# Beginning of a one-core program: zero products, first projection by parts, squares on ScalarE, early norm rows, streamed tokens for beta and the decay

## The chip, the cores and the metric

The kernel runs on one core of one Trainium2 chip. The core has a matrix engine (TensorE, PE in the profile) and three engines for element-wise work: VectorE (DVE), ScalarE (ACT) and GpSimd (POOL). SyncE (SP) issues transfers. Each engine takes its instructions in the order in which the program holds them, and waits on semaphores for what other engines and transfers deliver. The metric is the time of one execution on the device in microseconds; lower is better.

## The reference

256 tokens of width 1024 pass through a hybrid layer and then, with 16 learned tokens put in front of them, through two layers of a second kind. Only the mixer of the hybrid layer is touched by the change:

```python
def hybrid_layer(x, ...):
    h = rmsnorm(x, norm_mix_w)
    proj = h @ w_in                       # 1024 -> 3*512 (q, k, v), 512 (z), 4 (beta), 4 (a), 512 (lru_x), 512 (lru_gate)
    qkv, z, b_logit, a_logit, lru_x, lru_gate = split(proj)
    qkv = silu(causal_depthwise_conv(qkv, gdn_conv_w))        # 4 taps
    q, k, v = split(qkv); q = l2norm(q); k = l2norm(k)        # 4 heads of 128
    beta = sigmoid(b_logit); g = -exp(gdn_A_log) * softplus(a_logit + gdn_dt_bias)
    o = gated_delta_rule_chunked(q, k, v, g, beta)            # a triangular solve per chunk, a state from chunk to chunk
    gdn_out = rmsnorm(o, gdn_norm_w) * silu(z)
    hr = rg_lru(causal_depthwise_conv(lru_x, lru_conv_w) + lru_conv_b, ...)   # h[t] = a[t] h[t-1] + sqrt(1 - a[t]^2) i[t] x[t], two sigmoid gates
    lru_out = hr * gelu(lru_gate)
    x = x + concat(gdn_out, lru_out) @ w_out
    return x + square(relu(rmsnorm(x, norm_mlp_w) @ w_ff1)) @ w_ff2
```

The second block has, twice, a SwiGLU MLP, a mixer of attention and convolution, and another SwiGLU MLP.

## The kernel before, in words

**Products.** Features lie on the partitions and tokens are the 256 moving columns. Each operand is split into a rounded high part and the rest. The weights stream in by transfers on SyncE's queue into three buffers `raw`; ScalarE rounds a piece of 1024 columns to `wh`, and VectorE subtracts to get the low part `wl` (GpSimd does that for some kinds of projections, which the table `POOLED` names). Activations are held the same way: `x.hi` and `x.lo`. For each of the eight blocks of the inner dimension, `job` (line 525) issues three products into one bank of PSUM:

```python
nc.tensor.matmul(acc, h[:, s], xh, start=first and done == 0, stop=False)
nc.tensor.matmul(acc, h[:, s], xl, start=False, stop=False)
nc.tensor.matmul(acc, lo[:, s], xh, start=False, stop=last and done == total - 1)
```

One *projection* here is 24 such products, for 128 output features and all tokens. The mixer has 24 of them, in the order of `ORDER1`: four each for k, q, lru_x, lru_gate, v, z.

**Flows and the planner.** What follows a projection is written as generators (*flows*). A planner keeps an estimated clock for each engine (`clk`) and, after each step of a projection (`tick`), lets a flow go on when its inputs are due by that clock. So each engine's program order comes out of estimated costs, start values (`clk.update`), ranks of flows and limits.

**The beginning.** The tokens come into `H`. `first_norm` (line 750) makes `x.hi` on ScalarE and `x.lo` on VectorE for each of the eight blocks; the norm's factor per token is not in it, it is applied after the projections. `squares` (line 728) squares the tokens: four blocks on ScalarE, four on GpSimd, and GpSimd adds them to four accumulators. `tok_sums` (line 608) sums over features by products with a column of ones (one moving column; a float32 product takes several passes and is one or more rows in the trace), `root_norm` makes the factor `rc` per token, and `to_rows` (line 617) spreads it to a row `R`, equal on all partitions, by three products with the identity in the mask tile `M`. `R` is what each projection's result is multiplied with first.

**Behind a projection.** `conv4` (line 783) multiplies the bank with `R` into a buffer of the `arena` (a space for passing tiles, first come first served), clears the three columns ahead of it on GpSimd, lets ScalarE take the first tap and VectorE the other three (`scalar_tensor_tensor`, three *convolution steps*). `twice_silu` follows. For q and k the squares for the l2 norm are taken on GpSimd.

**The decay.** `decays` (line 885) gets beta and the decay's logit: the 16 columns `wb` (high and low part of 8 weight columns) are the moving operand and the tokens are stationary, 32 narrow products. VectorE adds the parts, a chain of small steps gives softplus, `nA` = -exp(A_log), and `G`, the log-decay per token and head. GpSimd multiplies `G` with a triangular mask into `DT`, two products spread it, and from that come the decay masks and factors of the chunks. `factors` (line 988) makes the norm factors of k and q; `bk` is the first of them, needed by the chunks.

**The chunks.** `chunk(0)` and `chunk(1)` handle 128 tokens each: transposes (*flips*) of k, the triangular matrix, its inverse in four levels of small blocks, whose last step is the 64x64 products against the masks `LM`, then U (16 products), the outputs, their root mean square `sso`, the normed output `on`, two flips back, and the gating with z into `mx`.

**The recurrence.** `lru` (line 1249) takes four tiles of lru_x: a gate product (`LG`), tanh, exponentials, a square root for all four tiles, then for each tile a multiply, a scan over tokens, a multiply with the gelu gate, and the split into `mx` (ScalarE the high part, VectorE the low).

**The end of the mixer.** w_out is applied in two halves: `o1a` the inner blocks 4 to 7 (recurrence tiles 0 to 3), 96 products into four banks, each opened by a product of zeros with 512 columns; `o1b` the blocks 0 to 3 (the chunks' output), into the same banks. From `o1b` on come the MLP and the second block.

## Time and profile before

| | us |
|---|---|
| time, median of 3 runs | 1510.01 (1508.57 to 1511.97) |
| time of the profiled execution | 1510.12 |
| its span in the profile | 1508.4 |
| TensorE busy | 98% |
| VectorE busy | 71% |
| ScalarE busy | 53% |
| GpSimd busy | 9% |

A line in a row of the profile is that of the helper that records the operation (`mm`, `tt`, `stt`, `act`, ...), "out<-in" are the program's names, and the number after the x counts instructions. A row of stretches gives for each engine its busy time with the number of instructions, then the clock granted to TensorE as a share of full speed, and what the transfers did.

### The profile page before, as it was taken

The numbers are of one execution on the slowest core, as the hardware profiler recorded it, in microseconds if no ns is written. First come the engines' busy times: TensorE is split into PE (matmuls) and PEld (weight loads), VectorE is DVE, ScalarE is ACT, GpSimd is POOL, SyncE is SP. The second block draws the span as 40 slices with busy tenths as digits, with TensorE's granted clock in tenths as the row PEclk, the third lists the DMA queues.
The fourth block names the chain that finished last, engine by engine and source line by source line (L and its number), as shares of the span: only waits on it lengthen the run. The fifth ranks groups of instructions, "written<-read, shape, count | busy, mean of one in ns | idle before, by whom it ended". The sixth has DMA issues, their size and how long they took to land. (4 is left out here: it accounts for less than half of the span.)

```text
span 1508.4 us, 29363 instructions
## 1 busy us (share of the span) xinstructions
PE 1471.4 (98%) x12130; PEld 1451.6 (96%) x12130; DVE 1073.8 (71%) x1910; ACT 800.6 (53%) x1349; POOL 136.7 (9%) x189
## 2 busy tenths in 40 slices
PE   7989999999999999999999999999999999999997
PEld 7888999999999999998999999999999989999997
DVE  5996877667666568998866655665568998876664
ACT  4568666544544445554554444544445556555552
POOL 2330300001000002231000000000002222000000
PEclk8999999999999999999999999999999999999998
DMA  5412455554644554333454444554454434555552
GB/s 207 163 57 73 164 205 190 187 200 145 209 170 176 178 177 144 144 134 112 147 214 171 173 169 161 199 185 174 165 190 155 164 113 140 184 207 196 189 183 76
DMA packets 36375, 248.57 MB, mean 165 GB/s; under 512 B 3984, under 2 KB 5264, under 8 KB 12304
## 3 DMA queue, kind: packets, MB, share of 16 engines
q1 hardware_dynamic: 35248, 245.50, 46.3%
q8 instruction: 95, 1.56, 0.4%
q10 hardware_dynamic: 992, 1.19, 0.2%
q14 instruction: 40, 0.33, 0.1%
HBM read 245.63 MB, written 1.05 MB: 164 GB/s over the span
## 5 line engine op out<-in xcount | busy, mean ns | idle before, releaser
L552 PE MATMUL bank<-x,wh 128*128 128x272 f32 (+1 forms) x2752 | 793.3, 288 | 11.0 <-ACT x L295 10.1
L553 PE MATMUL bank<-x,wh 128*128 128x272 f32 (+1 forms) x2752 | 782.8, 284 | 3.8 <-DVE x L318 2.2
L554 PE MATMUL bank<-x,wl 128*128 128x272 f32 (+1 forms) x2752 | 781.7, 284 | 4.4 <-DVE wl L307 4.4
L307 DVE TENSOR_TENSOR wl<-raw,wh 128x1024 fp32r<-128x1024 f32 (+3 forms) x467 | 546.6, 1172 | 182.7 <-PE bank L554 153.9
L295 ACT ACTIVATE wh<-raw 128x1024 fp32r<-128x1024 f32 (+4 forms) x494 | 492.1, 1001 | 255.3 <-issue 133.0
L552 PEld LDWEIGHTS bank<-x,wh 128*128 128x128 f32 x2752 | 521.5, 190 | 13.8 <-ACT x L295 10.5
L553 PEld LDWEIGHTS bank<-x,wh 128*128 128x128 f32 x2752 | 521.4, 189 | 6.9 <-DVE x L318 3.1
L554 PEld LDWEIGHTS bank<-x,wl 128*128 128x128 f32 x2752 | 521.9, 190 | 5.5 <-DVE wl L307 5.5
L554 PE MATMUL bank<-hid,wl 128*128 128x272 f32 (+1 forms) x960 | 270.5, 282 | 0.0
L552 PE MATMUL bank<-hid,wh 128*128 128x272 f32 (+1 forms) x960 | 270.5, 282 | 0.0
L553 PE MATMUL bank<-hid,wh 128*128 128x272 f32 (+1 forms) x960 | 270.5, 282 | 0.0
L553 PEld LDWEIGHTS bank<-hid,wh 128*128 128x128 f32 x960 | 180.5, 188 | 0.0
L554 PEld LDWEIGHTS bank<-hid,wl 128*128 128x128 f32 x960 | 180.5, 188 | 0.0
L552 PEld LDWEIGHTS bank<-hid,wh 128*128 128x128 f32 x960 | 180.5, 188 | 0.0
L307 DVE TENSOR_TENSOR tmp<-bank,R 128x272 f32<-128x272 f32 (+1 forms) x184 | 78.7, 429 | 63.5 <-PE bank L554 61.3
L295 ACT ACTIVATE tmp<-tmp 128x272 f32<-128x272 f32 (+1 forms) x140 | 59.4, 425 | 110.0 <-DVE tmp L307 78.0
L318 DVE SCALAR_TENSOR_TENSOR bank<-arena,C,bank 128x272 f32<-128x272 f32 (+1 forms) x232 | 102.3, 489 | 3.7 <-ACT bank L295 2.5
L510 POOL TENSOR_TENSOR wl<-raw,wh 128x1024 fp32r<-128x1024 f32 (+1 forms) x27 | 64.2, 2380 | 185.2 <-ACT wh L295 106.6
L307 DVE TENSOR_TENSOR hid<-tmp,hid 128x272 fp32r<-128x272 f32 (+1 forms) x120 | 51.7, 432 | 38.1 <-ACT hid L295 38.1
L295 ACT ACTIVATE hid<-tmp 128x272 fp32r<-128x272 f32 (+1 forms) x120 | 51.0, 426 | 42.3 <-DVE tmp L307 40.8
L295 ACT ACTIVATE x<-H,C 128x272 fp32r<-128x272 f32 (+2 forms) x64 | 30.0, 487 | 80.9 <-DVE H L307 80.3
L307 DVE TENSOR_TENSOR tmp<-tmp,bank 128x272 f32<-128x272 f32 (+1 forms) x88 | 38.0, 432 | 39.0 <-ACT tmp L295 39.0
(205 smaller groups left out, 883.2 us busy)
## 6 DMA issues: line engine op xcount, KB each, us to landing
raw<-in_w_dram SPq DMA_DIRECT2D x187, 1024.0 KB, 4.8
raw<-in_w_dram SPq DMA_DIRECT2D x32, 960.0 KB, 4.7
raw<-in_w_dram SPq DMA_DIRECT2D x16, 896.0 KB, 4.5
raw<-in_w_dram SPq DMA_DIRECT2D x2, 512.0 KB, 5.9
H<-in_xt_dram SPq DMA_DIRECT2D x1, 544.0 KB, 6.6
LG<-in_lgw_dram SPq DMA_DIRECT2D x1, 512.0 KB, 6.2
out_dram<-H SPq DMA_DIRECT2D x2, 256.0 KB, 2.2
LM<-in_cm_dram SPq DMA_DIRECT2D x1, 320.0 KB, 5.4
```

The lines of the kernel that those rows point to most:

```text
L295: nc.scalar.activation(out, in_, func, scale=scale, **kw)
L307: nc.vector.tensor_tensor(out=out, in0=a, in1=b, op=fn)
L318: nc.vector.scalar_tensor_tensor(out=out, in0=a, scalar=s, in1=b, op0=op0, op1=op1)
L510: nc.gpsimd.tensor_tensor(out=lo[:, a:a + n], in0=raw[c][:, o:o + n], in1=wh[i][:, a:a + n].bitcast(F32), op=SUB)
L552: nc.tensor.matmul(acc, h[:, s], xh, start=first and done == 0, stop=False)
L553: nc.tensor.matmul(acc, h[:, s], xl, start=False, stop=False)
L554: nc.tensor.matmul(acc, lo[:, s], xh, start=False, stop=last and done == total - 1)
```

## The change

- **Zero products.** The tile of zeros is made at the start, on 128 partitions; `WARM` = 13 products of 512 columns on it run while inputs come, and one after each of the first seven products of projection 0.
- **Projection 0 by parts.** Instead of three products per block, all eight `wh` with `x.hi`, then all eight `wl` with `x.hi`, then all eight `wh` with `x.lo`.
- **Squares on ScalarE.** All eight blocks, with no additions: `tok_sums` runs over eight accumulators instead of four. ScalarE rounds the second piece of weights ahead of them.
- **Norm rows at once.** `to_rows` is issued before the table load for exponentials and before `hrc`.
- **Streamed tokens for beta.** `wb` is now the stationary operand and the 256 tokens move, high and low, 16 products into 16 partitions; ScalarE copies the result, and two products with `two` (identity halves added) add the parts and turn the result back.
- **Decay earlier.** `decays` starts behind the first projection instead of the second and with another rank; `DT` is made on ScalarE in eight steps.
- **Convolutions.** Six fixed buffers, cleared once, instead of a new one with its own clearing; the squares of q and k go to ScalarE; the low weight parts of K and Q are no longer given to GpSimd. The pad of `hid` grows, and the planner's start values change.

```diff
--- before
+++ after
@@ -26,2 +26,4 @@
 SHARED = ("ys", "yc")
+WARM = 13
+CONVB = 6
 LEAD = 3
@@ -35,3 +37,3 @@
 AHEAD = 0.5
-POOLED = [(("a", "b", "q", "k", "v", "gc", "gs"), 4), (("yc",), 2), (("o1b",), 2), (("K", "Q"), 8)]
+POOLED = [(("a", "b", "q", "k", "v", "gc", "gs"), 4), (("yc",), 2), (("o1b",), 2)]
 LIMIT1 = 1.5
@@ -545,2 +547,15 @@
             clk["P"] = max(clk["P"], w_at[i] + LAT)
+            if u == 0:
+                for w, part in ((h, x.hi), (lo, x.hi), (h, x.lo)):
+                    for i, k in enumerate(units[u][1]):
+                        nc.tensor.matmul(
+                            acc, w[:, 128 * i:128 * i + 128], part(k), start=part == x.hi and w is h and i == 0,
+                            stop=part == x.lo and k == KD - 1,
+                        )
+                        if w is h and part == x.hi and k < KD - 1:
+                            mm(free_banks[-1], zero[:, 0:128], zero)
+                clk["P"] = 12.3
+                main.t, main.eng = clk["P"], "P"
+                tick()
+                continue
             for i, k in enumerate(units[u][1]):
@@ -702,2 +717,4 @@
     warm = const.tile([128, 1], F32, name="warm")
+    zero = pool1.tile([128, 512], BF16, name="zero")
+    nc.gpsimd.memset(zero, 0.0)
     nc.gpsimd.memset(ones, 1.0)
@@ -714,3 +731,5 @@
     emit_dma(2)
-    clk.update(P=6.5, A=4.1, V=6.2, G=5.6, D=12.0)
+    for _ in range(WARM):
+        mm(free_banks[-1], zero[:, 0:128], zero)
+    clk.update(P=6.5, A=5.3, V=6.4, G=5.6, D=12.0)
     raw_t.update({0: 3.9, 1: 9.2, 2: 12.1})
@@ -726,20 +745,15 @@
     hrc = const.tile([128, 2], F32, name="hrc")
+    two = pool1.tile([16, 8], F32, name="two")
+    convb = [arena.get(T1 + 8) for _ in range(CONVB)]
+    for a in convb:
+        nc.gpsimd.memset(a.f[:, 5:8], 0.0)
+    conv_left = [16, CONVB]
 
     def squares():
-        yield "P"
-        for k in range(4):
-            act(SQ[1].f[:, k], X(4 + k), AF.Square)
-        cur[0].t, cur[0].eng = 0.0, "P"
-        for k in range(4):
-            pt(SQ[0].f[:, k], X(k), X(k), MUL)
-        for k in range(4):
-            pt(SQ[0].f[:, k], SQ[0].f[:, k], SQ[1].f[:, k], ADD)
-        nc.gpsimd.memset(mean512, 1.0 / 512)
-        nc.gpsimd.memset(onesrow, 1.0)
+        for k in range(KD):
+            act(SQ[k // 4].f[:, k % 4], X(k), AF.Square)
         yield "P"
         yield from take()
-        root_norm([SQ[0].f[:, k] for k in range(4)], T1, rc)
+        root_norm([SQ[k // 4].f[:, k % 4] for k in range(KD)], T1, rc)
         note(ev_rc)
-        ts(hrc, rc, 0.5, MUL)
-        act(warm, ones[:, 0:1], AF.Exp)
         yield "P"
@@ -748,2 +762,4 @@
         note(ev_r1)
+        act(warm, ones[:, 0:1], AF.Exp)
+        ts(hrc, rc, 0.5, MUL)
 
@@ -759,3 +775,2 @@
     emit_high(0)
-    sq_flow = start_flow(squares())
     f = start_flow(first_norm())
@@ -766,4 +781,6 @@
         hop(f)
-    hop(sq_flow)
-    hop(sq_flow)
+    emit_high(1)
+    hop(start_flow(squares()))
+    nc.gpsimd.memset(mean512, 1.0 / 512)
+    nc.gpsimd.memset(onesrow, 1.0)
     ba = cv("w_ba").rearrange("p (a b) -> p a b", a=8)
@@ -771,2 +788,3 @@
     tt(wb[:, :, 8:16], ba, wb[:, :, 0:8].bitcast(F32), SUB)
+    tt(two, ident[0:16, 0:8], ident[0:16, 8:16], ADD)
     XR, GL = arena.get(4, T1), arena.get(4, T1)
@@ -784,5 +802,6 @@
         yield from wait(ev_r1)
-        pb = yield from room(T1 + 8)
+        while not convb:
+            yield "W"
+        pb = convb.pop(0)
         p = pb.f
-        nc.gpsimd.memset(p[:, 5:8], 0.0)
         tt(p[:, 8:8 + T1], b[:, 0:T1], R[:, 0:T1], MUL)
@@ -796,3 +815,8 @@
             stt(out, p[:, 5 + k:5 + k + T1], cv(wname, 4 * t + k), out, MUL, ADD)
-        pb.done()
+        conv_left[0] -= 1
+        if conv_left[0] < conv_left[1] or conv_left[0] < 10 and conv_left[1] > 4:
+            conv_left[1] -= 1
+            pb.done()
+        else:
+            convb.append(pb)
 
@@ -810,3 +834,3 @@
             yield from twice_silu(dst, dst)
-            pt(SQ[t // 4].f[:, t % 4], dst, dst, MUL)
+            act(SQ[t // 4].f[:, t % 4], dst, AF.Square)
             note(ev_sqk[t])
@@ -892,16 +916,17 @@
         b = free_banks.pop(0)
+        for k in range(KD):
+            mm(b[0:16, 0:T1], wb[:, k], xa.hi(k), k == 0, False)
+            mm(b[0:16, 0:T1], wb[:, k], xa.lo(k), False, k == KD - 1)
+            clk["P"] += 0.1
+        bas = yield from slot()
+        cp(bas[0:16, 0:T1], b[0:16, 0:T1])
+        yield "P"
         for c in range(2):
-            for k in range(KD):
-                mm(b[:, 16 * c:16 * c + 16], xa.hi(k)[:, hs(c)], wb[:, k], k == 0, False)
-                mm(b[:, 16 * c:16 * c + 8], xa.lo(k)[:, hs(c)], wb[:, k, 0:8], False, k == KD - 1)
+            mm(b[:, 256 + 8 * c:264 + 8 * c], bas[0:16, hs(c)], two)
+        free_tmps.append(bas)
         yield from wait(ev_rc)
-        b2 = b[:, 0:32].rearrange("p (a b c) -> p a b c", a=2, b=2)
-        ba2 = small.tile([128, 2, 8], F32, tag="ba2", name="ba2")
-        vcopy(ba2, b2[:, :, 0])
-        tt(ba2, ba2, b2[:, :, 1], ADD)
-        give(b)
-        b = ba2.rearrange("p a b -> p (a b)")
         for c in range(2):
-            stt(x12[:, 4 * c:4 * c + 4], b[:, 8 * c + 4:8 * c + 8], rc[:, c:c + 1], cv("gdn_dt_bias"), MUL, ADD)
-            act(beta[:, 4 * c:4 * c + 4], b[:, 8 * c:8 * c + 4], AF.Tanh, scale=hrc[:, c:c + 1])
+            stt(x12[:, 4 * c:4 * c + 4], b[:, 260 + 8 * c:264 + 8 * c], rc[:, c:c + 1], cv("gdn_dt_bias"), MUL, ADD)
+            act(beta[:, 4 * c:4 * c + 4], b[:, 256 + 8 * c:260 + 8 * c], AF.Tanh, scale=hrc[:, c:c + 1])
+        give(b)
         ts(x12[:, 8:12], cv("lru_a_param"), -1.0, MUL)
@@ -928,3 +953,4 @@
         for c in range(2):
-            pt(DT[c].f, bh(tri), bc(G[:, 4 * c:4 * c + 4]), MUL)
+            for h in range(4):
+                act(DT[c].f[:, h], tri, AF.Copy, scale=G[:, 4 * c + h:4 * c + h + 1])
         yield "P"
@@ -970,4 +996,2 @@
     junk = pool1.tile([128, 128], F32, name="junk")
-    zero = pool1.tile([1, 512], BF16, name="zero")
-    nc.gpsimd.memset(zero, 0.0)
 
@@ -1286,4 +1310,4 @@
         start_flow(doers[c](b, off + t), *((0, LIMIT0) if c in "kq" else (2, LIMIT1)))
-        if i == 1:
-            start_flow(decays(), 1)
+        if i == 0:
+            start_flow(decays(), 0.5)
         if i == 6:
@@ -1335,3 +1359,3 @@
         b = free_banks.pop(0)
-        mm(b, zero[:, 0:128], zero, stop=False)
+        mm(b, zero[0:1, 0:128], zero[0:1], stop=False)
         for i in range(2):
@@ -1350,3 +1374,3 @@
     phase = ExitStack()
-    hid = XS(T1, FF1, phase.enter_context(tc.tile_pool(name="ff1", bufs=1)), "hid", pad=(56, 0))
+    hid = XS(T1, FF1, phase.enter_context(tc.tile_pool(name="ff1", bufs=1)), "hid", pad=(88, 0))
 
...
```

**How the order moves.** Two places, the beginning and the first `o1a` tile, in rows of the two programs; rows in between that only repeat are left out. `x_117` and `x_118` are `x.hi` and `x.lo`, `x_119` and `x_120` those of `mx`.

TensorE at the start, before: the second and the third step of projection 1 (bank 79) with the norm's sums between them.

```order
L554 MATMUL bank_78<-x_117,wl 128x256
L552 MATMUL bank_79<-x_117,wh 128x256
L553 MATMUL bank_79<-x_118,wh 128x256
L554 MATMUL bank_79<-x_117,wl 128x256
L338 MATMUL bank_80<-ones,arena 128x1 x8
```

The same place with the change, from the last products of projection 0 to the row spread (bank 82, from `rc`).

```order
L340 MATMUL bank_85<-zero 128x512
L551 MATMUL bank_78<-x_117,wh 128x256
L551 MATMUL bank_78<-x_117,wl 128x256 x8
L551 MATMUL bank_78<-x_118,wh 128x256 x8
L567 MATMUL bank_79<-x_117,wh 128x256
L568 MATMUL bank_79<-x_118,wh 128x256
L569 MATMUL bank_79<-x_117,wl 128x256
L340 MATMUL bank_80<-ones,arena 128x1 x16
L340 MATMUL bank_81<-x_117,wb 16x256
L340 MATMUL bank_82<-M,rc 128x128
L340 MATMUL bank_82<-M,rc 128x64 x2
L340 MATMUL bank_81<-two,tmp_86 128x8 x2
```

The sums stand at the same place of projection 1, after one step of it, but there are twice as many; the products for beta and the row spread, which stood in projection 2, now stand in projection 1.

VectorE at the same time with the change: from the parts of `x.lo` to the end of the decay's chain (`sp`, `G`).

```order
L320 SCALAR_TENSOR_TENSOR x_118<-H,C,x_117 128x256 x6
L309 TENSOR_TENSOR wb<-C,wb 128x8x8
L309 TENSOR_TENSOR two<-M 16x8
L309 TENSOR_TENSOR wl<-raw,wh 128x1024 x3
L320 SCALAR_TENSOR_TENSOR rc<-rn_t,rn_y 128x2
L314 TENSOR_SCALAR hrc<-rc 128x2
L309 TENSOR_TENSOR arena<-bank_78,R 128x256
L320 SCALAR_TENSOR_TENSOR x_292<-bank_81,rc,C 128x4 x2
L309 TENSOR_TENSOR G<-sp_196,nA 128x8
L320 SCALAR_TENSOR_TENSOR arena<-arena,C 128x256 x2
```

The first multiplication with `R` has moved ahead of the decay's chain, and the second one (bank 79, not shown) stands behind it.

ScalarE with the change, from the first rounding of tokens to the exponential of the decay's chain.

```order
L297 ACTIVATE x_117<-H,C 128x256 x8
L297 ACTIVATE wh<-raw 128x1024
L297 ACTIVATE arena<-H 128x256 x8
L297 ACTIVATE wb<-C 128x8x8
L297 ACTIVATE rn_y<-bank_80,eps 128x2
L297 ACTIVATE tmp_86<-bank_81 16x256
L297 ACTIVATE R<-bank_82 128x256
L297 ACT_TABLE_LOAD
L297 ACTIVATE warm<-ones 128x1
L297 ACTIVATE arena<-arena,C 128x256
L297 ACTIVATE beta<-bank_81,hrc 128x4 x2
L297 ACTIVATE e_293<-e_293 128x12
```

Before, four squares stood here instead of eight, `R` came after the decay's `nA` instead of ahead of the table load, and no convolution stood ahead of beta.

TensorE at the first `o1a` tile, before (bank 81), from the product that opens it.

```order
L338 MATMUL bank_81<-zero 128x512
L552 MATMUL bank_81<-x_119,wh 128x256
L553 MATMUL bank_81<-x_120,wh 128x256
L554 MATMUL bank_81<-x_119,wl 128x256
L338 MATMUL bank_84<-arena 128x128 x4
L338 MATMUL bank_83<-arena 128x128 x4
L338 MATMUL bank_80<-arena 128x128 x4
L338 MATMUL bank_82<-arena 128x128 x4
L338 MATMUL bank_79<-arena 128x128 x8
L338 MATMUL bank_85<-arena 128x128 x8
```

The same place with the change (bank 79); bank 85 and bank 81 in the last rows are the two flips of the chunks' outputs.

```order
L340 MATMUL bank_79<-zero 128x512
L340 MATMUL bank_81<-arena 128x128 x4
L340 MATMUL bank_83<-arena 128x128 x4
L567 MATMUL bank_79<-x_119,wh 128x256
L340 MATMUL bank_78<-arena 128x128 x4
L340 MATMUL bank_84<-arena 128x128 x4
L340 MATMUL bank_80<-arena 128x128 x8
L567 MATMUL bank_79<-x_119,wh 128x256
L340 MATMUL bank_82<-arena 128x128 x8
L567 MATMUL bank_79<-x_119,wh 128x256
L344 MATMUL bank_85<-M,arena 128x128 x4
L344 MATMUL bank_81<-M,arena 128x128 x4
```

Before, eight steps were in the queue by the end of the second group of eight, and the flips came behind the 15th and the 17th. With the change one step stands ahead of the first eight, the third (recurrence tile 2) behind all of them, and the flips come right behind the third.

VectorE at that place with the change: `sso` is the outputs' root mean square, the last `x_120` rows are the low parts of recurrence tiles 2 and 3 (128x256) and of the two gated chunk outputs (128x4x128).

```order
L309 TENSOR_TENSOR sso<-sso,fq 128x4
L309 TENSOR_TENSOR arena<-bank_82,sso 128x512
L309 TENSOR_TENSOR arena<-bank_84,sso 128x512
L309 TENSOR_TENSOR x_120<-arena,x_119 128x256
L320 SCALAR_TENSOR_TENSOR arena<-bank_85,hw,arena 128x512
L320 SCALAR_TENSOR_TENSOR arena<-bank_81,hw,arena 128x512
L336 SCALAR_TENSOR_TENSOR arena<-arena 128x256
L309 TENSOR_TENSOR x_120<-arena,x_119 128x4x128 x2
L309 TENSOR_TENSOR x_120<-arena,x_119 128x256
L309 TENSOR_TENSOR wl<-raw,wh 128x512 x7
```

Before, all four recurrence tiles' `x_120` rows stood ahead of the first `sso` step; now tiles 2 and 3 stand among and behind the steps of the chunks' outputs. From `o1b` on the rows of TensorE are the same in both programs.

4 lines of the change are left out of this document (2 added, 2 removed).

## The prediction

> **What bounds the kernel now.** I read the page first, then the waits of TensorE, then a table of stretches, and then the rows of the queues in order of time. All times are microseconds.
>
> ```profile
> PE 1471.4 (98%) x12130; PEld 1451.6 (96%) x12130; DVE 1073.8 (71%) x1910; ACT 800.6 (53%) x1349; POOL 136.7 (9%) x189
> ```
>
> TensorE is the bound: it is busy nearly always. From the first `o1b` product on, the change leaves the order of every engine as it was, so what counts is when TensorE gets there: 163.8 (the last `zero` product at 160.69, 0.32 for it, 24 products). I split the way at three marks: the fourth projection (32.3), the end of the last 64x64 product (131.8), and `o1b` (163.8).
>
> ```profile
> core 0: us, PE busy (x) PEld busy (x) DVE busy (x) ACT busy (x) POOL busy (x), PEclk, DMA share, GB/s
> 16.10:17.50 1.40, 1.40 (x14) 1.40 (x14) 1.40 (x2) 0.73 (x1) 0.00 (x0) 1.00 0.67 94
> 18.20:23.90 5.70, 5.70 (x28) 5.70 (x29) 2.01 (x7) 2.70 (x4) 0.00 (x0) 0.50 0.75 315
> 24.40:27.60 3.20, 3.20 (x30) 3.20 (x31) 0.00 (x0) 0.00 (x0) 0.00 (x0) 1.00 0.02 5
> 27.80:31.10 3.30, 3.30 (x17) 3.30 (x16) 2.53 (x16) 0.79 (x4) 0.00 (x0) 0.50 0.00 0
> 31.70:39.40 7.70, 7.70 (x68) 7.70 (x69) 6.04 (x12) 3.60 (x6) 4.62 (x6) 1.00 0.60 221
> ...
> 67.90:131.80 63.90, 58.38 (x574) 55.44 (x572) 50.77 (x92) 46.55 (x105) 17.48 (x19) 1.00 0.23 81
> 131.80:143.10 11.30, 10.87 (x89) 10.07 (x88) 10.71 (x26) 9.11 (x20) 0.00 (x0) 1.00 0.26 94
> 143.10:152.10 9.00, 8.92 (x79) 8.69 (x78) 4.98 (x12) 7.77 (x23) 0.00 (x0) 1.00 0.33 117
> 152.10:163.80 11.70, 11.68 (x91) 10.40 (x90) 10.40 (x29) 6.71 (x18) 1.77 (x1) 1.00 0.14 34
> ```
>
> A projection product of 256 columns takes 0.113 at clock 1.00 (68 in 7.70) and 0.21 at 0.50 (27 of the 28 in 5.70). The clock drops to 0.50 after the one-column sums (16.1 to 17.5) and after the narrow `wb` products (24.4 to 27.6), though TensorE shows as busy in both, and it comes back only after several microseconds of wide products. In the last three stretches TensorE has no gap worth naming: the serial end of the two chunk flows lies under 72 projection products and the `o1a` products.
>
> ```profile
> PE bank L342 <- DVE arena L307: 2.5, 2, 1.8
> PE bank L554 <- DVE wl L307: 2.1, 2, 1.2
> ```
>
> Its waits between 32.3 and 131.8 are small: these two lead, 7.5 in all by the rows of that view. That is the most that a better fed TensorE can win there.
>
> **The change, part by part.** The sum is made against the profiled execution, 1510.12 (span 1508.4, 1.7 around it); the median of the runs is 1510.01, so no correction is needed.
>
> *Start to fourth projection.*
>
> ```profile
> 6.57 2.69 POOL L330 TENSOR_TENSOR arena<-H 128x256 f32<-128x256 f32 x4 [5.53 <-DMA H<-in_xt_dram]
> 6.59 3.45 ACT L295 ACTIVATE x<-H,C 128x256 fp32r<-128x256 f32 x8 [0.35 <-DMA H<-in_xt_dram]
> 9.95 1.32 ACT L295 ACTIVATE arena<-H 128x256 f32<-128x256 f32 x4
> 10.26 3.98 DVE L318 SCALAR_TENSOR_TENSOR x<-H,C,x 128x256 fp32r<-128x256 f32 x5
> ...
> 14.70 3.48 DVE L307 TENSOR_TENSOR wl<-raw,wh 128x1024 fp32r<-128x1024 f32 x3
> 16.18 2.15 PE L338 MATMUL bank<-ones,arena 128*128 128x1 f32 x16
> 24.10 3.77 PE L338 MATMUL bank<-wb,x 128*128 128x16 f32 x32
> 29.34 0.17 DVE L312 TENSOR_SCALAR nA<-nA 128x4 f32<-128x4 f32 x1 [0.29 <-ACT nA L295]
> 30.39 1.31 PE L338 MATMUL bank<-M,rc 128*128 128x128 f32 x6
> 31.73 0.39 ACT L295 ACTIVATE R<-bank 128x256 f32<-128x256 f32 x1 [2.43 <-PE bank L338]
> 32.22 0.17 DVE L307 TENSOR_TENSOR G<-sp,nA 128x8 f32<-128x8 f32 x1
> ```
>
> The 13 zero products cost nothing: x arrives at 6.6, and 13 times 0.43 (512 columns at half clock) from about 1.4 ends at 7.0. The eight between the first products cost nothing either: even at half clock, 0.64 a step ends at 12.2, and the step after them waits longer. With squares off GpSimd, VectorE's x parts run at about 0.45 instead of 0.8 (3.98 for five, beside GpSimd), so projection 0 ends near 12.3. But the next low half (`wl` of projection 1) now stands behind `wb` on VectorE, and `wb` behind eight squares on ScalarE: 10.04, plus 1.0 (`wh`), plus 8 x 0.33, plus 0.24 is 13.9; VectorE adds 0.35 and 1.15: 15.4. Before, TensorE got this at 15.96. So 0.5 is won of what seemed 3, and TensorE idles 3 in the middle.
>
> Then the sums: eight accumulators instead of four, 32 passes for 16. A pass is 0.10 at full clock (14 in 1.40), about 0.21 at half. With 3 idle and then one-column sums the clock must fall as it did at 17.5; I take 12 passes at full and 20 at half, ending near 21.5 (bounds 19.0 and 22.3). Now 25 wide products, 16 of them `wb` with 256 moving columns, at half clock take 5.3 (26.8), the row spread 1.2, and the clock returns about there; the two small `two` products 0.4; then 36 products at 0.113, 4.1: the fourth projection starts at **32.5**, against 32.3. If the clock never fell: 15.5 + 3.4 + 61 x 0.113 + 1.5 = 27.3; if it never came back before the mark: 15.5 + 6.7 + 61 x 0.21 + 1.6 = 36.6. I take 32.5, since the rows show the fall after less idling than this.
>
> The Trainium skill, "TensorE: Matmul & The Clock Gate", Part 1 (What's actually happening), says that the half clock is the default, that a free-running window of 3.4 with sustained work lifts it, and that an idle window brings it back; so warmth bought before 7 is lost again in the idle stretch after 12.3, as the 0.50 stretches here suggest.
>
> *Norm rows to the chunk flows.* The row spread ends at 28.0, R is copied at 28.4 instead of 32.1. But on ScalarE a table load (1.28), `warm`, a convolution start and beta now stand between R and `e`, some 2.8 in all, and on VectorE all decay steps stand ahead of the second convolution step. From `nA` to the end of `G` VectorE took 3.05 (29.34 to 32.39); so G ends at about 34.5, 2.1 later than before. R's lead is spent waiting.
>
> ```profile
> 38.10 3.52 DVE L318 SCALAR_TENSOR_TENSOR arena<-arena,C 128x256 f32<-128x256 f32 x3
> ...
> 63.75 1.39 DVE L318 SCALAR_TENSOR_TENSOR arena<-arena,C 128x256 f32<-128x256 f32 x3
> ```
>
> From G on VectorE is full until the norm factors `bk`. It is given one more `wl` (1.15), and loses GpSimd's company: three convolution steps took 3.52 beside a GpSimd subtraction, 1.39 alone. By its new order: 24 convolution steps x 0.44, 10 `wl` x 1.15, 15 multiplies and silus x 0.35, 3.0 for the decay rows, 2.3 for a root: 32, so `bk` is ready at 66.5 (67.8 before). TensorE reaches its first chunk flip at about 67 (67.87 before), with 14.1 projections behind it instead of 13.5. The first steps of the chunks then follow closer (18 products stood between them, now 6), another 1.5. From there to the last 64x64 product both orders hold about as many projection products (180 and 177) and the same chunk steps. So this mark comes **2.5 earlier, at 129.3** (bounds: 120.5, if nothing were ever cold and every wait vanished; 134, if the late G is passed on in full).
>
> *The end of the mixer.* Here the order has turned against the kernel. What was under 72 + 96 products is left with 60 + 96, and in the new order the first `o1a` tile wants recurrence tiles 1, 2 and 3, which VectorE makes inside and behind the chunks' last steps.
>
> ```profile
> 127.09 0.84 ACT L295 ACTIVATE tmp<-bank,hb 128x256 f32<-128x256 f32 x2
> 127.83 1.08 ACT L295 ACTIVATE arena<-tmp,n 128x256 f32<-128x256 f32 x2
> 134.02 1.28 ACT L295 ACT_TABLE_LOAD   x1
> 135.32 1.07 ACT L295 ACTIVATE arena<-arena 128x1024 f32<-128x1024 f32 x1
> 141.85 2.16 ACT L295 ACTIVATE arena<-bank,hbeta 128x128 f32<-128x128 f32 x8
> ...
> 136.88 0.69 DVE L334 TENSOR_TENSOR_SCAN arena<-arena 128x256 f32<-128x256 f32 x1
> 151.77 0.16 DVE L307 TENSOR_TENSOR sso<-sso,fq 128x4 f32<-128x4 f32 x1 [3.54 <-ACT junk L295]
> 154.22 0.16 DVE L307 TENSOR_TENSOR sso<-sso,fq 128x4 f32<-128x4 f32 x1
> 154.49 0.69 DVE L307 TENSOR_TENSOR arena<-bank,sso 128x512 f32<-128x512 f32 x1
> ...
> 143.16 1.95 PE L338 MATMUL bank<-arena 128*128 128x128 f32 x16
> 150.39 1.95 PE L338 MATMUL bank<-arena 128*128 128x128 f32 x16
> ```
>
> Counting from the mark: gate product 0.95, two tanh 0.85, two exponentials 1.08, a tanh 0.5, two weight roundings 1.2, two tanh 0.7, table 1.28, root 1.0, table 1.28, tanh 0.3, four `hbeta` scalings 1.1. U starts at +10.3 (before: 143.16, +11.4). From U to the first `sso` step 8.6 (143.16 to 151.77), its chain 2.6 (151.77 to 154.4). Then, new on this path: recurrence tile 2 on VectorE 1.5, ScalarE's rounding of it 0.5, and only behind that the second chunk's squares 1.6; second chain 1.1; two `on` 1.3; tile 2's low half 0.35. Only now `o1a`'s third step can run, with the two flips 1.4; gating 0.7; tile 3 1.5; three low halves 1.75. That is 22.9 after U, and then 87 `o1a` products (9.8) and three zero products (1.0) are still to do, with nothing to hide. 10.3 + 22.9 + 10.8 = 44.0, against 32.0: **+12.0**. TensorE stands idle about 8.5 in one piece, from the last chunk output (U + 8.9) to the third step (U + 17.5).
>
> ```profile
> 700.60:704.60 4.00, 1.05 (x7) 0.81 (x6) 2.97 (x6) 2.75 (x5) 2.34 (x1) 0.88 0.17 37
> 704.60:710.40 5.80, 5.77 (x20) 5.02 (x21) 2.77 (x7) 3.95 (x8) 0.00 (x0) 0.50 0.43 167
> ```
>
> The same kernel shows what such a gap costs behind it: after 4.0 with 1.05 of work, the clock was 0.50 for another 5.8, half of it lost: 2.9. I take **+2.6** (bounds 1.7 and 3.4).
>
> By the skill's window of 3.4 alone, the half clock would last 3.4 to 6.8 after work resumes, a loss of 1.7 to 3.4; the row lies inside, so the sum would not change.
>
> The pad of `hid`, the six fixed convolution buffers and the decay rows on ScalarE (8 x 0.27 for 2.96 on GpSimd) lie beside VectorE's full stretch: nothing, and with that cover gone at most their 2.2.
>
> Sum: -2.5 + 12.0 + 2.6 = +12.1, from 1510.1 to **1522**.
>
> **The rivals.** (1) *A shorter tail.* ScalarE and VectorE may reach the mark with work already done that I put behind it, and the mark may come at 126. The tail then costs half: -5.5 + 7 + 2.2 = about +4, 1514. For it: ScalarE is busy 46.55 of 63.90 before the mark; against it: its queue is in order and the root stands behind the last gate. (2) *Even.* The clock falls shorter at the start (fourth projection at 29) and the tail is as in (1): 1510, 1507 to 1513. (3) *Faster.* One mechanism: the clock stays up from the zero products on. Then the fourth projection starts at 27.3, R comes 5 earlier, VectorE's stretch shifts by 5, saved contention adds 3, and the mark lies near 121; with a tail of half the price the end is 163.8 - 10.5 + 7 = 160, so about 1506, and 1503 with less tail. It decides from a mark below 122. For it: sustained wide products gave 1.00 from 31.7 on; against it: the idle stretch and 32 narrow passes, after which this trace shows 0.50. (4) *The change does not do what it says*: R spread at once, yet all convolutions behind G; that is in my sum already.
>
> **How the numbers follow.** Forecast (a tail of 9 to 15 and a cold clock behind it) 0.57, own range 1516 to 1529; (1) 0.15; (2) 0.10; (3) 0.18. A measurement of this kernel tells about 0.2% (3) from no change. Slower is the forecast and (1): 0.72; same 0.10; faster 0.18. The range 1506 to 1529 leaves out the lower half of (3) and what lies above a full tail with a late mark, together near 0.2.
>
> **What would show it.** Right: sums near 15.5 with the clock at 0.50 soon after; G at 33 to 36; the last 64x64 product at 127 to 132; TensorE idle 10 or more between that and `o1b`, released by VectorE's `x` and `arena` rows, then a stretch at 0.50; `o1b` near 176. Wrong: clock 1.00 from 8 to 32, or TensorE without gaps after the mark, or `o1b` before 164.

## The result, and the profile after

The changed kernel takes 1536.24 (median of 4 runs, 1534.88 to 1538.17) against 1509.29 for the kernel before: a ratio of 1.0174, interval 1.0159 to 1.0189. Measured again with more runs it was 1536.64 against 1510.2, ratio 1.0161 (1.0132 to 1.0191). So it is slower, as forecast, but by 26 to 27 instead of 12, and outside the range, whose upper end was 1529.

The profiled execution has a span of 1534.4 against 1508.4. At the prediction's marks the 26.0 split like this:

| | before | predicted | after | against before |
|---|---|---|---|---|
| fourth projection starts | 32.4 | 32.5 | 30.6 | -1.8 |
| last 64x64 product ends | 131.9 | 129.3 | 133.7 | +1.8 |
| from there to the first `o1b` product | 31.8 | 46.6 | 49.3 | +17.5 |
| from `o1b` to the end | 1344.7 | 1344.7 | 1351.4 | +6.7 |

The 46.6 is the prediction's 44.0 plus 2.6 for the cold clock (cold: granted 0.50, half speed). The last three rows of the last column add up to the 26.0.

**The start.** A table of stretches of the changed kernel shows the sums (15.3 to 20.6), the half clock around them, the way to the first flip of the chunks, to the second matrix A, and to the last 64x64 product.

```profile
core 0: us, PE busy (x) PEld busy (x) DVE busy (x) ACT busy (x) POOL busy (x), PEclk, DMA share, GB/s
15.30:20.60 5.30, 5.30 (x34) 5.30 (x33) 2.02 (x2) 1.13 (x2) 0.00 (x0) 0.65 0.80 294
16.90:23.70 6.80, 6.80 (x33) 5.97 (x33) 2.35 (x8) 0.26 (x1) 0.00 (x0) 0.50 0.73 282
30.60:66.40 35.80, 35.10 (x292) 33.94 (x291) 34.23 (x86) 22.59 (x46) 3.73 (x4) 1.00 0.46 159
66.40:81.20 14.80, 11.36 (x70) 10.35 (x69) 5.94 (x20) 9.10 (x26) 0.00 (x0) 0.79 0.28 104
81.20:133.70 52.50, 50.81 (x500) 47.82 (x499) 42.14 (x72) 35.16 (x74) 10.98 (x8) 0.99 0.23 81
```

The sums start at 15.3 and run mostly at half clock, as forecast; the clock comes back at 23.7, earlier than the prediction had it. From 30.6 to 66.4 VectorE is full (34.23 of 35.80). The first flip comes at 66.4. Then the lead is lost: 14.8 pass until VectorE starts on the second of the chunks' two triangular matrices (the second A, below), with a mean clock of 0.79. The same stretch before, and the one behind it:

```profile
67.90:79.30 11.40, 9.60 (x82) 9.04 (x81) 9.26 (x28) 9.37 (x24) 4.64 (x7) 1.00 0.45 172
79.30:131.90 52.60, 48.88 (x495) 46.48 (x494) 41.60 (x65) 37.28 (x82) 12.84 (x12) 1.00 0.18 61
```

11.4 became 14.8, and from the second A to the last 64x64 product both kernels need the same: 52.6 and 52.5.

**The end of the mixer.** TensorE's waits in the changed kernel, first as groups between 133 and 184 (total, times, longest), then its rows in order of time; the number in brackets is the idle time before the row, with what ended it.

```profile
PE bank L567 <- ACT x L297: 7.8, 3, 4.2
PE bank L568 <- DVE x L309: 4.4, 2, 3.9
PE bank L340 <- ACT arena L297: 2.0, 2, 1.7
```

```profile
144.73 2.15 PE L340 MATMUL bank<-arena 128*128 128x128 f32 x16 [1.73 <-ACT arena L297]
...
153.05 1.83 PE L340 MATMUL bank<-arena 128*128 128x128 f32 x14 [0.24 <-ACT arena L297]
159.11 0.39 PE L567 MATMUL bank<-x,wh 128*128 128x256 f32 x1 [4.24 <-ACT x L297]
163.40 0.58 PE L568 MATMUL bank<-x,wh 128*128 128x256 f32 x1 [3.90 <-DVE x L309]
163.78 0.42 PE L569 MATMUL bank<-x,wl 128*128 128x256 f32 x1
163.99 1.91 PE L344 MATMUL bank<-M,arena 128*128 128x128 f32 x8
168.71 0.58 PE L567 MATMUL bank<-x,wh 128*128 128x256 f32 x1 [2.81 <-ACT x L297]
169.80 0.58 PE L568 MATMUL bank<-x,wh 128*128 128x256 f32 x1 [0.51 <-DVE x L309]
```

These are the rows that the prediction spoke of: U at 144.7, the outputs, then the third `o1a` step, which gets its high part at 159.1 and its low part at 163.4, and the fourth at 168.7 and 169.8. Only then do the other `o1a` products follow. VectorE's rows show why: `x` at 162.93 is the low part of recurrence tile 2, and it stands behind both chains of `sso`.

```profile
154.48 0.16 DVE L309 TENSOR_TENSOR sso<-sso,fq 128x4 f32<-128x4 f32 x1 [3.54 <-ACT junk L297]
...
160.54 0.16 DVE L309 TENSOR_TENSOR sso<-sso,fq 128x4 f32<-128x4 f32 x1 [1.93 <-ACT junk L297]
...
161.72 1.29 DVE L309 TENSOR_TENSOR arena<-bank,sso 128x512 f32<-128x512 f32 x2
162.93 0.42 DVE L309 TENSOR_TENSOR x<-arena,x 128x256 fp32r<-128x256 f32 x1
165.09 1.60 DVE L320 SCALAR_TENSOR_TENSOR arena<-bank,hw,arena 128x512 f32<-128x512 f32 x2 [1.75 <-PE bank L344]
```

**Behind `o1b`.** Here both kernels have the same instructions in the same order, and still 6.7 lie between them. Stretches of the changed kernel: the half clock behind the idle time, everything from `o1b` on, and 120 in the midst of the two MLP products that follow the mixer.

```profile
164.00:173.10 9.10, 5.78 (x25) 4.86 (x24) 5.18 (x9) 2.42 (x5) 0.00 (x0) 0.50 0.00 0
183.10:1534.40 1351.30, 1331.72 (x10909) 1319.61 (x10907) 947.57 (x1639) 698.58 (x1128) 98.75 (x132) 1.00 0.48 169
...
240.00:360.00 120.00, 120.00 (x1021) 120.00 (x1020) 78.15 (x129) 67.19 (x112) 0.00 (x0) 1.00 0.53 188
```

The same of the kernel before:

```profile
163.80:1508.40 1344.60, 1325.57 (x10909) 1313.48 (x10907) 947.52 (x1640) 698.71 (x1128) 97.78 (x132) 0.99 0.49 170
...
220.00:340.00 120.00, 120.00 (x1062) 120.00 (x1061) 80.73 (x131) 69.30 (x114) 0.00 (x0) 1.00 0.56 196
```

TensorE is busy throughout at a granted clock of 1.00, and yet it did 1021 products in 120 in the one kernel and 1062 in the other: 0.1175 and 0.1130 each. The single rows have 117.8 ns against 113.3 ns, product after product. The last 1377 of the 1536 products of these two matrices run without a break, from 214.7 to 376.9 in the changed kernel and from 195.6 to 351.7 in the kernel before: 162.2 against 156.1. That is 6.1 of the 6.7; 0.5 more is one wait just ahead of them that is longer (0.7 against 0.2).

### The profile page after: what moved, and what is told of

It reads as the page before. It is cut to its first block, busy times and chain, and to the rows that moved or that the text cites. A ratio compares the mean times of both kernels' runs of the same rounds, so it can differ in the third digit from the quotient of the medians.

```text
span 1534.4 us, 29387 instructions
## 1 busy us (share of the span) xinstructions
PE 1490.6 (97%) x12154; PEld 1463.7 (95%) x12154; DVE 1067.7 (70%) x1910; ACT 808.3 (53%) x1370; POOL 116.2 (8%) x160
## 5 line engine op out<-in xcount | busy, mean ns | idle before, releaser
L309 DVE TENSOR_TENSOR wl<-raw,wh 128x1024 fp32r<-128x1024 f32 (+4 forms) x468 | 545.9, 1168 | 196.7 <-PE bank L569 165.2
```

Of the source, the lines that this page charges most:

```text
L309: nc.vector.tensor_tensor(out=out, in0=a, in1=b, op=fn)
```

## The experiments

The theory: the planner, started from other costs and clocks, made an order with too little TensorE work left for the end of the mixer; the operations of the change cost little in themselves. The rival: the operations moved to VectorE and ScalarE cost the time, whatever the order. Where only the planner was touched, every operation of the change is still there. The times of two variants can differ by 6 to 7 through the pace behind `o1b` alone, so the start of `o1b` in the profiles is the cleaner measure; the table at the end of this section has it, with the pace in its last column.

**No zero products.**

```diff
-WARM = 13
+WARM = 0
-                        if w is h and part == x.hi and k < KD - 1:
-                            mm(free_banks[-1], zero[:, 0:128], zero)
```

> The changed kernel without its zero products (13 while inputs come, 7 in projection 0); the order of everything else is the same. Theory A (the zero products are hidden): projection 0 ends a little later than 12.3, but TensorE waited 2.5 for the low half of projection 1 until 15.1 anyway, so the sums start within 0.5 of 15.3 and the time stays within 2 of 1536. Theory B (they hold the clock up): without them the clock is 0.50 longer at the start, the fourth projection starts 3 or more later than 30.6 and the time rises to 1539 or more. In both the granted clock of the 13 to 24 stretch is about 0.57, as in the changed kernel.

Measured: 1534.07 (1532.29 to 1543.1), ratio 1.0146 (1.0110 to 1.0183). The fourth projection starts at 30.4, against 30.6 with them: theory A at the start, where the zero products are hidden, and the clock falls after the sums in either case. That the time is near 1536 as well is in part luck: this profile has the quicker pace behind `o1b` (1345.6 against 1351.4). Further on `o1b` starts at 185.9 against 183.1 and 184.1 in the two profiles with them; whether these 2 to 3 come from the missing products or from where the half clock happened to fall, one profile does not tell. (Its half clock on the way to the second A lasted longer, as shown further down.)

**One number of the planner.**

```diff
-                clk["P"] = 12.3
+                clk["P"] = 13.2
```

> The changed kernel with one number of the planner changed: its clock for TensorE after projection 0 is 13.2 instead of 12.3. No operation is added, taken away or moved to another engine; only the order comes out differently. Theory A (the loss is the order that the planner happened to make, with too little work left beside the end of the chunks and the recurrence): the idle 17 between the last 64x64 product and the first o1b product shrinks by ten or more, o1b starts near 170 instead of 183, and the time is 1519 to 1527. Theory B (the moved operations themselves load VectorE and ScalarE, so any order pays): o1b stays within 4 of 183 and the time is 1531 to 1540.

Measured: 1516.05 (1508.76 to 1519.06), ratio 1.0013 (0.9993 to 1.0034). Theory A, and more than it said (1519 to 1527). With the same operations and one number different, the time is 20 lower: the way from the last 64x64 product to `o1b` is nearly as full as in the kernel before.

```profile
75.60:128.10 52.50, 49.48 (x488) 46.53 (x487) 41.40 (x72) 36.90 (x78) 11.69 (x8) 1.00 0.19 64
128.10:162.50 34.40, 32.47 (x261) 30.43 (x261) 25.48 (x64) 26.39 (x61) 1.69 (x1) 1.00 0.24 88
220.00:340.00 120.00, 120.00 (x1021) 120.00 (x1020) 78.08 (x129) 67.04 (x112) 0.00 (x0) 1.00 0.53 188
```

The last 64x64 product ends at 128.1, `o1b` starts at 162.5, both earlier than before; the third row has the slower pace, and with the quicker one this profile would lie below that of the kernel before (an estimate: 162.5 + 1344.7 = 1507.2 against 1508.4). The number changed the start too. In this order the one-column sums follow projection 0 directly, at 12.0, and not at 15.3 behind the step that waits for its low half:

```profile
12.04 3.63 PE L340 MATMUL bank<-ones,arena 128*128 128x1 f32 x32
```

The half clock after them lasted 3.4 instead of 6.8, and the fourth projection starts at 26.0 instead of 30.6. Of the 20.6 that `o1b` comes earlier, these 4.6 are the start and 14.9 the tail (34.4 against 49.3); how much of the 4.6 is the order and how much the position of the half clock is not separated.

**The decay flow at its old place.**

```diff
-        if i == 0:
-            start_flow(decays(), 0.5)
+        if i == 1:
+            start_flow(decays(), 1)
```

> The changed kernel with the decay flow started behind the second projection with its old rank, as before the change; all operations stay. Theory A (order): the narrow products and G move a projection later, the chunks find more projections left beside their end, o1b starts near 165 to 170, time 1514 to 1524. Theory B (operations): within 5 of 1536. Theory C (an early G is worth something by itself, as the change means it): with G later the chunks start later and the time rises above 1538.

Measured: 1511.55 (1509.96 to 1514.36), ratio 0.9989 (0.9973 to 1.0005), a little better than theory A had it. G comes at 37.1 instead of 32.4, the last 64x64 product only at 137.4, and still `o1b` starts at 164.7: recurrence tiles 0 to 2 have left VectorE by 144.3, ahead of the outputs' first mean square (146.7), and tile 3 by 151.8, where the changed kernel had tiles 2 and 3 at 163.4 and 169.7. TensorE has 0.45 of idle time behind the mark instead of 14.3:

```profile
137.40:164.70 27.30, 26.85 (x219) 25.22 (x219) 20.11 (x53) 19.39 (x53) 1.05 (x1) 1.00 0.23 78
```

An early G was worth nothing here (theory C falls), and a late mark need not cost anything.

**A low weight part back on GpSimd.**

```diff
-POOLED = [..., (("yc",), 2), (("o1b",), 2)]
+POOLED = [..., (("yc",), 2), (("o1b",), 2), (("K", "Q"), 8)]
```

> The changed kernel with one low weight part of the k and q projections given back to GpSimd, as before the change. Theory A (order, changed by anything): the tail's idle time shrinks by 10 or more, time 1518 to 1528. Theory B (VectorE's load ahead of the norm factors is what is late): bk becomes ready 1.2 earlier than 66.0, everything behind it follows by about as much, and the time is 1533 to 1536. Theory C (GpSimd beside VectorE slows its steps): bk is not earlier, time 1536 or more.

Measured: 1519.13 (1516.96 to 1525.87), ratio 1.0043 (1.0021 to 1.0066). Theory A again. `bk` came at 67.2, not earlier, so it was not VectorE's load ahead of `bk` that changed the time: `o1b` starts at 171.0.

**The tail alone.** Here the order is untouched up to the place that the prediction named.

```diff
-        yield from wait(ev_fq)
+        yield from wait(ev_fq, *mx.ev[4:8])
         so = sso[:, sc]
```

> The changed kernel with one wait in the planner: the mean squares of the chunks' outputs may start only when all four recurrence tiles are in the queues. TensorE's order is the same up to the flips of the outputs in the first o1a tile, which move behind o1a work; no operation changes. Theory A (the prediction's tail: the third o1a step waits for a recurrence tile that stands behind the second output's mean square on VectorE): the o1a products run from about 152 without the waits of 4.24, 3.90 and 2.81, the half clock of 160 to 174 is gone, o1b starts 8 to 14 earlier than 183, the time is 1522 to 1530. Theory B (the outputs' own chain is what o1b waits for, whatever stands in front): o1b starts within 4 of 183 and the wait only moves to the first o1b product, time 1532 to 1540.

Measured: 1517.87 (1516.3 to 1524.65), ratio 1.0054 (1.0028 to 1.008). Theory A: `o1b` starts at 170.4, 12.7 earlier. The time lies below the range of theory A because four of the seven runs, and so the median, are in the lower group (1516.3 to 1517.87, the others 1523.66 to 1524.65); the profiled run, with the slower pace like that of the changed kernel, took 1523.88 against 1536.6. TensorE's waits between 134 and 172, and the stretch up to `o1b`:

```profile
PE bank L340 <- ACT arena L297: 2.1, 2, 1.9
PE bank L569 <- DVE wl L309: 0.7, 1, 0.7
PE bank L567 <- ACT x L297: 0.5, 1, 0.5
...
155.50:170.40 14.90, 13.62 (x103) 11.94 (x102) 11.44 (x33) 8.48 (x27) 1.78 (x1) 1.00 0.17 57
```

The waits of 7.8 and 4.4 have shrunk to 0.5, the clock is 1.00 from 155.5 on, and the outputs' own chain (`sso`, gating) ends in time. The place is shown: recurrence tiles 2 and 3 behind the outputs' mean square on VectorE cost some 13. The way from the mark to `o1b` is 36.2 here, still 4.4 more than before the change; that rest was not followed up.

**Zero products in the waits.** It was made to separate the idle time from the cold clock behind it.

```diff
+    def fill(b, count, first=False):
+        for _ in range(count):
+            nc.tensor.matmul(b, zero[:, 0:128], zero[:, 0:b.shape[-1]], start=first, stop=first)
+                if j == 24 and i in (2, 3):
+                    fill(acc, 38 if i == 2 else 24)
+                if j == 24 and i == 2:
+                    fill(acc, 34)
...
+        if c == 1:
+            fill(b, 4, True)
+        if c == 0:
+            fill(b, 9, True)
```

> The changed kernel with zero products put where TensorE waited: 4 and 9 of 512 columns ahead of the second and third flip of the chunks (waits 0.91 and 1.95), and in the first o1a tile 38, 34 and 24 of 256 columns ahead of its third step, inside it, and ahead of the fourth (waits 4.24, 3.90, 2.81). The order of all else is the same. Theory A (the cold clock behind a wait costs, +2.6 in the prediction for the tail and about 3 for the stretch of 71 to 82): the granted clock stays 1.00 from 25 on, the last 64x64 product ends near 131, o1b starts 47 later instead of 49.3, and the time falls by 4 to 6. Theory B (the waits themselves are the loss, a cold clock only fills them): the mark and o1b move by less than 1.5 each, time within 2.5 of the changed kernel.

Measured: 1528.64 (1528.57 to 1535.27), ratio 1.0131 (1.0097 to 1.0166).

```profile
82.10:134.80 52.70, 50.83 (x500) 47.79 (x500) 42.19 (x72) 35.29 (x74) 10.97 (x8) 1.00 0.23 81
...
25.50:134.80 109.30, 103.91 (x922) 96.86 (x921) 84.65 (x188) 71.40 (x155) 14.70 (x12) 1.00 0.29 105
134.80:181.50 46.70, 42.47 (x339) 38.18 (x340) 25.37 (x63) 26.02 (x62) 1.28 (x1) 1.00 0.13 46
```

The clock is 1.00 all the way. In the tail the way from the mark to `o1b` falls from 49.3 (and 50.2 in the second profile of the changed kernel) to 46.7: the cold clock cost 2.6 to 3.5 there, the prediction took 2.6. Most of the 7.6 in the time is not that, but the quicker pace behind `o1b` in this profile (1345.1 against 1351.4).

Between the first flip and the second A the run does not show what a warm clock is worth. The second A comes at 82.1, against 81.2 and 81.4 without the zero products, but nine of these did not land in the wait of 1.95. They stand behind the one-column sums, where TensorE had work, and took 1.9 of its time:

```profile
75.07 1.95 PE L340 MATMUL bank<-ones,arena 128*128 128x1 f32 x16
76.88 1.89 PE L529 MATMUL bank<-zero 128*128 128x512 bf16 x8
```

Other profiles answer it. From the first flip to the second A the changed kernel, its second profile, the run without zero products, the interrupted kernel (below) and the run with the recurrence first have the same instructions in the same order on TensorE, VectorE and ScalarE. Only the half clock fell differently. The second profile, the run without zero products and the interrupted kernel:

```profile
67.80:81.40 13.60, 10.16 (x69) 8.98 (x68) 5.93 (x20) 9.10 (x26) 0.00 (x0) 0.87 0.30 114
```

```profile
66.20:82.70 16.50, 13.27 (x71) 12.31 (x71) 5.99 (x21) 9.28 (x26) 0.00 (x0) 0.69 0.23 90
```

```profile
67.90:84.90 17.00, 14.15 (x70) 13.12 (x70) 5.89 (x20) 9.27 (x26) 0.00 (x0) 0.60 0.25 91
```

With the changed kernel's own row, and 13.6 at 0.87 again with the recurrence first, the way is 13.6, 14.8, 16.5 and 17.0 as the clock falls from 0.87 to 0.79, 0.69 and 0.60. Warm, it would be about 12.3 (an estimate: 14.2 with the zero products, less their 1.9), against 11.4 in the kernel before. So of the 3.4 that the changed kernel lost there, about 0.9 goes with the new order itself and about 2.5 with the half clock.

**The side steps later.** They stand between the two chunks' first steps.

```diff
-        yield from wait(ev_fx, *ev_q)
+        yield from wait(ev_fx, *ev_q, *ev_at)
...
         tt(AT.f, v4(b), DT[c].f, MUL)
+        note(ev_at[c])
```

> The changed kernel with one wait in the planner: the side steps of the chunks (flips and scalings of k and q) may start only when both chunks have their first matrix A. In the changed kernel these side steps stand between the first A (73.7) and the second (81.2); before they came 2.4 apart, and from the second A's first mask step to the last 64x64 product both kernels need 49 to 50. Theory A (the second A sets the last 64x64 product): the second A comes near 77, the last 64x64 product near 129.5. The tail behind it keeps its shape, so the time falls by about 4 if the tail is the same, and by more or less as its order changes: 1522 to 1533. Theory B (the first stretch is bound by something else, the norm factors or cold products): the last 64x64 product stays within 1.5 of 133.7.

Measured: 1529.9 (1527.81 to 1532.9), ratio 1.0131 (1.0096 to 1.0166). The edit did not do what it was made for: the planner filled the room with projections (115 TensorE products from the first flip to the second A, where the changed kernel has 70), the second A came at 86.7 and the last 64x64 product at 141.8. So it is no test of what held the second A back. It does show once more that mark and end are different things: the mark is 8 later, and `o1b` 2.4 earlier.

**One part alone, on the kernel before.** 13 zero products while inputs come; the order of all else stays.

```diff
...
+    for _ in range(13):
+        nc.tensor.matmul(free_banks[-1], zero[:, 0:128], zero, start=True, stop=True)
     clk.update(P=6.5, A=4.1, V=6.2, G=5.6, D=12.0)
```

> The kernel before with one part of the change alone: 13 zero products of 512 columns while inputs come. The order of all else is that of the kernel before. Theory A (worth nothing: the one-column sums bring the half clock back at about 17 whatever came before, and projection 0 is paced by the arriving tokens): the fourth projection starts within 1.5 of 32.4, time within 3 of the kernel before. Theory B (a warm start is worth its half clock): the fourth projection starts at 29 or earlier, time 3 or more below.

Measured: 1513.63 (1507.96 to 1515.23), ratio 1.0002 (0.9984 to 1.002): by time theory A. But its one profile shows theory B's place: the half clock lay at 9.2 to 16.0, still in projection 0, the fourth projection started at 27.7 and `o1b` at 161.2. What the parts at the start are worth beyond the half clock's chance position is left open.

**The pace.** Two runs: the changed kernel once more, with more runs of both kernels beside it, and the changed kernel with the stream of equal products interrupted.

```diff
+        opened = first and kind in ("ff1", "ff2")
+        if opened:
+            nc.tensor.matmul(acc, zero2[:, 0:128], zero2, start=True, stop=False)
+            first = False
...
```

> The changed kernel once more, unchanged, with many runs beside the kernel before. In the first profile the products of the two MLP projections after the mixer took 117.8 ns each, in the kernel before 113.3 ns, over 1536 products: 6.8. Theory A (a product's pace is drawn anew at an interruption of TensorE and then stays): both kernels show two groups of times some 6 apart, the changed kernel near 1530 and near 1536, the kernel before near 1510 and near 1516; the median difference is 20 to 26. Theory B (the pace belongs to the program, say to where its tiles lie): the changed kernel has one group, near 1536.

> The changed kernel with one zero product of 256 columns opening each projection of the two MLP matrices behind the mixer, to interrupt the stream of equal products (38 of them, about 5 in all). Theory A (the pace of 113.3 or 117.8 ns is set at an interruption and holds until the next): each projection shows one pace from its start to its end, and both paces occur among the 38. Theory B (the pace belongs to the place of the operands): all projections that read the same activations show the same pace.

Measured: the five runs of the changed kernel are 1530.57, 1531.55, 1536.64, 1537.95 and 1540.08; the 17 of the kernel before lie at 1508.06 to 1511.36 (14) and 1516.63 to 1518.48 (3). Theory A: two groups in both, though not equally often. Of the nine runs of the changed kernel seven are in its upper group, of these 17 of the kernel before three. The interrupted kernel took 1553.13 in its one run, and its profile shows the starts of the zero products, one per projection of 24:

```profile
226.67 0.28 PE L543 MATMUL bank<-zero 1*128 1x256 bf16 x1
...
229.82 0.28 PE L543 MATMUL bank<-zero 1*128 1x256 bf16 x1
...
233.05 0.28 PE L543 MATMUL bank<-zero 1*128 1x256 bf16 x1
...
236.20 0.28 PE L543 MATMUL bank<-zero 1*128 1x256 bf16 x1
```

The distances are 3.15, 3.23, 3.15, and so on: from there on projections at 113.3 and at 117.8 ns in turn, each one pace from start to end, all reading the same activations. So the pace belongs to how the stream was taken up after an interruption, not to the place of the activations; and without the interruptions the same weights and banks follow one another at one pace. The interruption itself costs 0.4 (3.15 less 24 times 0.1133), not the 0.1 that I had put for a product: about 16 for the 40 of them, where I had 5.

**An order for the changed operations.** The decay flow at its old place, and the planner's lead for low parts smaller.

```diff
-AHEAD = 0.5
+AHEAD = 0.2
```

> The changed kernel with the decay flow started behind the second projection, as in the run before it of that kind, and the planner's lead for low weight parts at 0.2 instead of 0.5; all operations of the change stay. It looks for an order that suits the changed operations. Theory A (with an order that leaves work beside the end of the chunks the beginning's gain of 2 to 6 shows): o1b near 163, less idle time in the second block, time 1503 to 1509. Theory B (the change's operations give nothing even with a good order): 1510 to 1515.

Measured: 1514.25 (1512.23 to 1521.56), ratio 1.0029 (1.0011 to 1.0047). Theory B by the time, and it does not settle the matter: the last 64x64 product came at 141.2 and `o1b` at 168.8, with the half clock at the start lasting from 16.4 to 30.1. No version of the changed kernel was found that beats the kernel before clear of its interval.

All profiles but that of the interrupted kernel by the marks of the prediction (from rows of the traces; the last column is the time from `o1b` to the end):

| | fourth projection | second A | last 64x64 product ends | `o1b` | to the end |
|---|---|---|---|---|---|
| before | 32.4 | 79.3 | 131.9 | 163.7 | 1344.7 |
| after | 30.6 | 81.2 | 133.7 | 183.1 | 1351.4 |
| after, again | 32.1 | 81.4 | 134.0 | 184.1 | 1351.7 |
| no zero products | 30.4 | 82.7 | 135.3 | 185.9 | 1345.6 |
| planner's number | 26.0 | 75.6 | 128.1 | 162.5 | 1350.8 |
| decay late | 32.2 | 81.6 | 137.4 | 164.7 | 1344.8 |
| low part on GpSimd | 32.0 | 81.0 | 133.9 | 171.0 | 1346.3 |
| recurrence first | 32.3 | 81.7 | 134.2 | 170.4 | 1351.3 |
| zeros in the waits | 32.1 | 82.1 | 134.8 | 181.5 | 1345.1 |
| sides later | 32.0 | 86.7 | 141.8 | 180.7 | 1345.1 |
| zeros alone | 27.7 | 76.7 | 129.4 | 161.2 | 1351.6 |
| decay late, lead 0.2 | 33.7 | 83.1 | 141.2 | 168.8 | 1345.0 |

## Why the prediction was right or wrong

- **The whole miss.** The profile has 26.0 where the sum had 12.1. The 13.9 between them are 4.3 at the mark, 2.9 in the tail and 6.7 behind `o1b`. Even the two fastest runs of the changed kernel (1530.57 and 1531.55) lie above the range's 1529.
- **The sign and its cause: right.** The prediction put the loss at the end of the mixer, with the third `o1a` step behind recurrence tile 2 and that behind the second output's mean square. The trace shows this chain, and the run with the recurrence first takes 13 of the loss back with that one edit.
- **The size of the tail: 2.9 too small.** Counted from the mark, U was to start at 10.3 and did at 11.0; the third step was to run at U + 17.5 and had its low part at U + 18.7; the fourth was ready at U + 25.1 instead of 22.9. Part of that is the flips, which took 1.91 at half clock. I had charged the cold clock only to what follows the idle time, not to the flips in its midst. The 2.6 for the cold clock was right by itself (2.6 to 3.5 measured).
- **The mark: the step that failed.** "The first steps of the chunks then follow closer ..., another 1.5" was wrong. The first flip came at 66.4 as forecast (67), `bk` at 66.0 (66.5), but 14.8 passed to the second A instead of 11.4. I had counted products between the steps and taken fewer for faster. With fewer between them TensorE waits 3.4 (11.36 busy of 14.80) for the steps' chain over ScalarE and VectorE, and then runs 6.3 of the 14.8 at half clock, a cost that I had charged only in the tail. By the profiles with the same order about 0.9 of the 3.4 lost is the order and about 2.5 the half clock (estimates); the gain of 1.5 would not have been there with a warm clock either. In nine of the twelve profiles of the table the time from the second A to the last 64x64 product is 52.5 to 52.9 (55 to 58 in the other three), so the late A went through in full: +1.8 instead of -2.5.
- **Behind `o1b`: not in the sum.** I took the same order for the same time. The pace made it 6.7 longer in this profile. Both kernels have both paces, so neither belongs to the change alone; whether it makes the slower one likelier (seven of nine runs against three of 17) is not shown. Within the lower group the kernels differ by about 21 (1530.57 and 1531.55 against 1508.06 to 1511.36), near the marks' 1.8 + 17.5 = 19.3.
- **The start: nearly right, for the reason given.** The sums at 15.3 (15.4 forecast) and the half clock around them came as said; it ended at 23.7 and not at 28, so the fourth projection started 1.9 earlier than forecast, G at 32.4 instead of 34.5. By `bk` 0.5 of that was left, and the second A was late all the same. Two sums of mine do not come out of their terms: 12 passes at 0.10 and 20 at 0.21 from 15.4 end at 20.8, not 21.5 (they ended at 20.6), and the terms from G to `bk` add up to 32.6, not 32.
- **The rivals.** (1) and (2) had a shorter tail; the tail was longer. (3), the clock up from the zero products on, did not come: 0.50 from 16.9 to 23.7. That one number of the planner makes a kernel level with the one before was in none of them: I priced one order, and did not ask how far it hung on the planner's start values.

## What to carry to other kernels

When a planner writes the order, a change is two things: its operations and the order that falls out. Run it with one start value of the planner nudged before judging the operations: here 0.9 on one clock was worth 20, with all operations equal, though part of it may be where the half clock fell. And look for the chain that ends a stage, then count the filler that is left beside it; an earlier start that spends the filler sooner can end later. Steps of a serial chain don't follow faster because less work stands between them; take the chain's own time as the floor, and price the half clock wherever idle time appears, not only at the largest gap.

## What the runs showed of the hardware

- **Two paces for equal products.** At a granted clock of 1.00, uninterrupted products of 256 columns take 113.3 or 117.8 ns, 4% apart, for more than 150 microseconds on end. Within an uninterrupted stream the pace held (1377 products on end in either kernel); where one small product opened each projection, it changed at these interruptions. From `o1b` to the end the twelve profiles of the table fall into 1344.7 to 1346.3 and 1350.8 to 1351.7, and the runs of one kernel into groups some 7 apart. What decides at the interruption is open.
- **The half clock comes in equal portions.** At the start it lasted 3.4 (planner's number), 6.8 (after), 10.2 (after, again) and 13.7 (lead 0.2):

```profile
16.20:19.60 3.40, 3.40 (x18) 2.33 (x17) 1.79 (x7) 0.78 (x1) 0.00 (x0) 0.50 0.85 308
```

```profile
15.30:25.50 10.20, 10.20 (x49) 9.14 (x49) 3.73 (x9) 1.17 (x2) 0.00 (x0) 0.50 0.55 207
```

```profile
16.40:30.10 13.70, 13.70 (x64) 12.83 (x65) 5.94 (x15) 3.87 (x7) 0.00 (x0) 0.50 0.39 154
```

Two profiles of the same program differ here by one portion (6.8 and 10.2), and the fourth projection by 1.5. The Trainium skill, "TensorE: Matmul & The Clock Gate", Part 1 (What's actually happening), has a free-running window of 3.4; by that rule the portions are windows and their position is chance. The trace agrees in the portion. So a single profile's start is one draw, and a gain of a few microseconds there needs several.
- **A one-product interruption cost 0.4**, nearly four times the 0.113 of a product in the stream.
- **A chain's length moved with the half clock.** The same instructions in the same order, from the first flip to the second A, took 13.6 to 17.0 as the mean granted clock went from 0.87 to 0.60.
